# Layer 0's modulation products on VectorE among the convolution's passes, and a first norm whose shift is made by TensorE

## Chip, core and metric

One core of a Trainium2 chip runs the whole program. Its engines are TensorE (PE in the profile, its weight loads are PEld), VectorE (DVE), ScalarE (ACT), GpSimd (POOL) and SyncE (SP), which here issues almost all DMAs. The metric is the time of one execution on the device in microseconds. Lower is better.

## What is computed

An encoder block of two layers on one sequence of 1024 tokens with 1024 channels, all in float32. Layer 0 mixes tokens by a Conformer convolution, layer 1 by a gated linear recurrence in both directions; each mixer is followed by a squared-ReLU MLP. Every sub-layer is normalised first and then modulated: shift, scale and gate come from a conditioning vector `c`. Cut to what matters here:

```python
cond = silu(c)                                   # (1, 1024)
for i in range(2):
    mod = cond @ ada_w[i] + ada_b[i]             # 6 parts of 1024 numbers per layer
    sh1, sc1, g1, sh2, sc2, g2 = split(mod, 6)   # parts 0 to 5
    h = rms_norm(x, norm1_g[i]) * (1 + sc1) + sh1
    y = conformer_conv(h) if i == 0 else hgrn2_mixer(h)
    x = x + g1 * y
    h = rms_norm(x, norm2_g[i]) * (1 + sc2) + sh2
    x = x + g2 * sq_relu_mlp(h)
return rms_norm(x, final_g)

def conformer_conv(h):
    a, gate = split(h @ w_in, 2)                 # w_in (1024, 2048)
    y = depthwise_conv(a * sigmoid(gate), width=31) + dw_b
    return silu(layer_norm(y)) @ w_out
```

## The kernel before

`x` lies as 8 tiles of 128 channels by 1024 tokens; `s` counts the two halves of 512 tokens and `b` the 8 blocks of channels. Every large product is made of three TensorE products of operands split into a high and a low part (`hi` by ScalarE, `lo` = value minus `hi` by VectorE or GpSimd); the weights are split in the same way (`prep_std`, lines 206 and 208).

**Modulation.** `ada` makes one part: for each of 8 blocks it loads a tile of the transposed `ada_w` (128 outputs by 1024 inputs, 512 KB, line 409), multiplies it by `cond` spread over all partitions and sums along the row. With `eng="vector"` one VectorE instruction does both (line 412) and `ada_done` follows for that block: it adds the bias (line 436) and for the scales forms `AB` (line 441). With `eng="gpsimd"` GpSimd multiplies (line 415) and ScalarE sums (line 418).

**Start.** `start` makes `cond`, loads `x`, sums its squares (`stages`, lines 528 and 531, then token sums on TensorE, line 489), takes the inverse root by a few small VectorE instructions (`newton`, lines 460 to 471) and spreads it over the partitions (line 484). Scale (part 1) goes by VectorE, shift (part 0) by GpSimd and ScalarE but for its last block. Then for each `b` the first half of the tokens goes by lines 557, 565 and 566, the second by `mod_split_pool` (lines 574 to 578) with its low part on GpSimd. The first two weight splits of the convolution (`PW`) are on GpSimd too.

**Convolution.** `conv_layer` runs two passes over the tokens (`PASS`: five, then three token tiles of 128) with four groups of 256 channels each. In each (pass, group), `conv_in` has four steps, one for each quarter of the input channels; a step is 2 x 3 TensorE products of 512 columns for each token tile (lines 726 to 728, 0.23 us apart at full clock). Between the steps of one group stand `forward` (a DFT of the group before, lines 759 to 761, filter by VectorE in line 766, sums by GpSimd in line 768, splits in 288 and 289, result `Y`) and `backward` (line 784). `setup_late` loads and splits the DFT matrices into the space of `x` once `x` has been read. `conv_norm` is the layer norm and swish of one half (lines 801 to 837): it runs for the first half among the second pass, and for the second half among `out_proj`, which multiplies by `w_out` (lines 268 to 272) and adds to `x` (line 711). Parts 2, 4 and 3 of layer 0 are made by GpSimd and ScalarE, one block for each step from the second pass on and the rest in `out_proj`.

The order on each engine is worked out ahead by a scheduler that plays the program on a model of the engines and takes ready instructions by their place in the program; `keep_in_program_order` pins an instruction behind the one written before it on its engine. At run time each engine takes its list in order. The raw weight tiles, and the tiles of parts 2, 4 and 3, share four buffers (`raw`).

Of the kernel before, what the change touches and what calls it, by code (L numbers as in the profile page):

```python
# [6 lines left out]
F32 = mybir.dt.float32  # L7
# [6 lines left out]
P = 128  # L14
# [62 lines left out]
AW = 12  # L77

PW = [("ci", 0, 0, 0), ("ci", 0, 0, 1), ("co", 3), ("co", 4)]
# [12 lines left out]
class K:  # L92
# [226 lines left out]
    def setup_late(self):  # L319
# [7 lines left out]
        self.Gm = sp.tile([P, 2, 2, G], F32R, name="Gm")  # L327
        raw = None
        for i in range(n + 2):
            if i % 4 == 0:  # L330
                raw = self.raw()
                w = min(4, n + 2 - i) * G
                nc.sync.dma_start(out=raw[:, 0:w], in_=self.ins["dft"][:, i * G:i * G + w])
            src = raw[:, i % 4 * G:(i % 4 + 1) * G]
            hi, lo = (self.F[i][:, e].rearrange("p c f -> p (c f)") if i < n else self.Gm[:, e, i - n] for e in range(2))
            nc.scalar.copy(out=hi, in_=src)
            nc.vector.tensor_tensor(out=lo, in0=src, in1=hi.bitcast(F32), op=ALU.subtract)
# [10 lines left out]
    def load_masks(self):  # L348

        nc = self.nc  # L350
        self.masks = self.cp.tile([P, len(LEVELS), P], U8, name="masks")
# [30 lines left out]
    def cond_rows(self, bufs):  # L382
# [7 lines left out]
        for s in range(2):  # L390
# [4 lines left out]
            ps = self.aux()  # L395
# [5 lines left out]
    def ada(self, layer, part, cond, tile, eng="vector", late=False):  # L401

        nc = self.nc
        for b in range(NB):
            if layer == part == 0 and b == NB - 1:
                eng = "vector"
# [4 lines left out]
            if eng == "vector":  # L411
                nc.vector.scalar_tensor_tensor(out=raw, in0=raw, scalar=1.0, in1=cond, op0=ALU.mult, op1=ALU.mult,
                                               accum_out=m)
# [7 lines left out]
            if layer == part == 0:  # L421
                nc.scalar.activation(out=m, in_=m, func=AF.Identity, bias=self.adab[:, b:b + 1])
            elif eng == "vector" or layer == part // 2 == 0:
# [3 lines left out]
            if not late:  # L427
                yield

# [45 lines left out]
    def spread(self, r, bank=None):  # L475
# [5 lines left out]
        for j in range(n):  # L481
            c = slice(j * P, (j + 1) * P)
            nc.vector.tensor_scalar(out=d[:, c], in0=self.ident, scalar1=r[:, j:j + 1], scalar2=None, op0=ALU.mult)
            nc.tensor.matmul(out[:, c], self.ones_m, d[:, c], start=True, stop=True)
# [36 lines left out]
    def stages(self, srcs, npool=0, ps=None, bank=None):  # L521
# [4 lines left out]
        for i, x in enumerate(srcs):  # L526
            sq = self.qp.tile([P, H], F32, tag="sq", name=self.nm("sq"))[:, 0:n]
# [33 lines left out]
    def mod_split(self, layer, n, b, t, h=None):  # L561
        shift = self.gcol(layer, 3 * n, b)
        if h is None:
            h = self.hp.tile([P, 2, H], F32R, tag="h", name=self.nm("h"))
# [4 lines left out]

    def mod_split_pool(self, layer, n, s, b, r, h):  # L570

        nc = self.nc
        t = self.t512("h")
        nc.vector.scalar_tensor_tensor(out=t, in0=self.x[b][:, self.hs(s)], scalar=self.AB[:, layer, n, b:b + 1],
                                       in1=r, op0=ALU.mult, op1=ALU.mult)
        nc.scalar.activation(out=t, in_=t, func=AF.Identity, bias=self.gcol(layer, 3 * n, b))
        nc.scalar.copy(out=h[:, 0], in_=t)
        nc.gpsimd.tensor_tensor(out=h[:, 1], in0=t, in1=h[:, 0].bitcast(F32), op=ALU.subtract)
        return h
# [94 lines left out]
    def start(self):  # L674
# [3 lines left out]
        for s in range(2):  # L678
            self.load_x(s)
        ps = self.aux()  # L680
        for s in range(2):
            sums, _, _ = self.stages(self.xs(s), ps=ps[:, 4 * s:])
            sums()
        r = self.newton(ps, 8)
        rs = [self.spread(r[:, 4 * s:4 * s + 4]) for s in range(2)]
        tile = lambda: self.ada_tile(AW)
        g1, g0 = self.ada(0, 1, cond, tile, "vector"), self.ada(0, 0, cond, tile, "gpsimd")
        h = [[self.hp.tile([P, 2, H], F32R, tag="h", name=self.nm("h")) for _ in range(NB)] for _ in range(2)]

        def block(b):  # L690
            for s in range(2):
                if s:
                    self.mod_split_pool(0, 0, s, b, rs[s], h[s][b])
                else:
                    t, _ = self.mod_scale(0, 0, s, b, rs[s])
                    self.mod_split(0, 0, b, t, h[s][b])
        for b in range(NB):
            next(g1)
            next(g0)
            if b == 1:  # L700
                self.prep(1)
            if b >= 2:
                block(b - 2)
        for b in range(NB - 2, NB):
            block(b)
        self.fetch(3)
# [144 lines left out]
    def conv_layer(self, h):  # L851
        nc, tc = self.nc, self.tc
        z = [[], []]
        with tc.tile_pool(name="y", bufs=2 * NB) as self.yp:
            Y, S, U = [[], []], [[], []], {}
            norm = iter(())
            gen = None
            with tc.tile_pool(name="conv", bufs=1) as self.sp:
                self.setup_late()
                prev = None  # L860
                for ps in range(2):
                    for g in range(NG):
                        ci = self.conv_in(ps, g, h, U)

                        def go():
                            next(ci)
                            for _ in range(ps):
                                next(norm, None)
                            if ps and gen:
                                next(gen, None)  # L870
# [5 lines left out]
                        if prev:  # L876
                            self.backward(*prev, F, Y[prev[0]], S[prev[0]])
                            if prev == (0, NG - 1):
                                norm = self.conv_norm(Y[0], S[0], 0, z[0])
                                cond = self.cond_rows(0)  # L880
                                gen = itertools.chain(*(self.ada(0, part, cond, self.raw, "gpsimd") for part in (2, 4, 3)))
# [9 lines left out]
            with tc.tile_pool(name="convout", bufs=6) as self.sp:  # L891
# [6 lines left out]
                def step():  # L898
                    for _ in range(2):
                        with tc.high_priority():  # L900
                            next(norm, None)
                        next(gen, None)
# [3 lines left out]
                for _ in gen:  # L906
                    pass
# [598 lines left out]
    def rest(self, z):  # L1506
        tc, nc = self.tc, self.nc
        B = {}
        with tc.tile_pool(name="mlp0", bufs=1) as self.sp:
# [8 lines left out]
            def step(n):  # L1518
                if n >= 8 and n % 2 == 0:
                    next(gen, None)  # L1520
                if n == 7:
                    self.load_masks()
# [10 lines left out]
    def part2(self, h2):  # L1533
# [4 lines left out]
        with tc.tile_pool(name="hgrn", bufs=2) as self.sp:  # L1538
            z = self.hgrn_layer(h2)
# [16 lines left out]
def _arrays(inputs):  # L1556
# [7 lines left out]
    a["ada_t"] = np.ascontiguousarray(w.transpose(0, 2, 1)).reshape(2 * 6 * D, D)  # L1564
    a["dw"] = np.ascontiguousarray(inputs["conv_dw_w"][0])
# [37 lines left out]
```

## Time and profile before

| | |
|---|---|
| time, median of 3 runs | 2524.74 us (2520.14 to 2525.76) |
| time of the profiled execution | 2520.98 us |
| its span, first to last instruction | 2519.2 us |
| TensorE busy | 2405.6 us, 95% |
| VectorE busy | 1812.9 us, 72% |
| GpSimd busy | 1008.1 us, 40% |
| mean granted TensorE clock | 0.984 |

Busy time is a mean over stages with different limits. The change touches the first 430 us alone, in which TensorE is busy for 363.91 us; they are read in five stretches: up to the first product of the convolution (0 to 42 us), to the first `forward` (97), to the second pass (205), to the end of its last `conv_in` (332), and to where the MLP's first inputs are made (430).

### The profile page before, as it was taken

The page shows a single profiled execution, that of the slowest core. Times are in us where ns is not written, and L with a number is a line of the kernel's source. Part 1 is how long each engine was busy: PE and PEld are TensorE (multiplying, and loading weights), DVE is VectorE, ACT ScalarE, POOL GpSimd, SP SyncE. Part 2 cuts the span into 40 slices and gives each one's busy share as a digit, 9 for nine tenths or more (in the row PEclk, how much of TensorE's full clock was granted, in tenths as well). Part 3 has the DMA queues.
Part 4 walks back from the last instruction along what each step waited for, and adds up shares of the span by engine and source line. Part 5 has one row for each costly group of instructions (what it writes and reads, how often), then busy time and mean ns, then how long its engine had stood idle before and what let it go on. Part 6 is the DMA issues. An engine that isn't in the chain of part 4 may idle for free.

```text
span 2519.2 us, 32120 instructions
## 1 busy us (share of the span) xinstructions
PE 2405.6 (95%) x12024; PEld 2014.3 (80%) x12024; DVE 1812.9 (72%) x2440; ACT 1012.3 (40%) x1706; POOL 1008.1 (40%) x554
## 2 busy tenths in 40 slices
PE   4999998899999999999999999999989999999998
PEld 3788876677788778889898898988867888888887
DVE  8646778877676998756767867677579666695564
ACT  5424554433334344433434434343333333343443
POOL 4225673476664976012111111010036666474321
PEclk9999998999999999999999999999999999999999
DMA  6223473154547656541112211122523444664554
GB/s 253 91 67 104 131 267 134 35 189 161 167 147 278 246 200 235 175 155 59 59 51 76 67 43 59 59 68 84 205 71 138 142 155 160 218 249 175 184 185 150
DMA packets 217106, 358.62 MB, mean 142 GB/s; under 512 B 14005, under 2 KB 118612, under 8 KB 216950
## 3 DMA queue, kind: packets, MB, share of 16 engines
q1 hardware_dynamic: 215222, 354.48, 40.9%
q8 instruction: 94, 1.54, 0.2%
q10 hardware_dynamic: 1728, 2.10, 0.2%
q14 instruction: 62, 0.51, 0.1%
HBM read 278.92 MB, written 77.60 MB: 142 GB/s over the span
## 4 chain that ended last, share of the span: by engine, by line
PE 77%; DVE 9%; DMA 5%; POOL 4%; issue 4%; ACT 1%; SPq 0%; POOLq 0%; DVEq 0%; ACTq 0%
PE acc L281 17%; PE acc L964 5%; PE acc L965 5%; PE acc L960 5%; PE aux L1232 4%; PE acc L1061 4%; PE acc L1066 4%; PE acc L1065 4%; PE aux L1061 3%; PE aux L1066 3%; PE aux L1065 3%; PE aux L960 2%; PE aux L964 2%; PE aux L965 2%; POOL raw L415 2%
## 5 line engine op out<-in xcount | busy, mean ns | idle before, releaser
L415 POOL TENSOR_TENSOR raw<-raw,cond 128x1024 f32<-128x1024 f32 x56 | 157.1, 2807 | 548.6 <-DMA raw<-in_ada_t 343.7
L281 PE MATMUL acc<-h,wh 128*128 128x512 f32 x1024 | 328.6, 397 | 0.0
L236 DVE TENSOR_TENSOR wp<-raw,wp 128x512 fp32r<-128x512 f32 x192 | 204.3, 1071 | 104.5 <-ACT wp L235 103.6
L964 PE MATMUL acc<-h,wp 128*128 128x512 f32 x640 | 255.2, 399 | 10.0 <-DVE h L633 10.0
L960 PE MATMUL acc<-h,wp 128*128 128x512 f32 x640 | 252.5, 401 | 8.6 <-ACT wp L235 3.4
L235 ACT CAST wp<-raw 128x512 fp32r<-128x512 f32 x192 | 117.5, 621 | 347.3 <-PE acc L965 170.0
L965 PE MATMUL acc<-h,wp 128*128 128x512 f32 x640 | 251.7, 399 | 0.7 <-DVE wp L236 0.7
L281 PEld LDWEIGHTS acc<-h,wh 128*128 128x128 f32 x1024 | 189.7, 188 | 36.7
L1049 DVE TENSOR_TENSOR o<-hold,o 128x1024 fp32r<-128x1024 f32 x80 | 151.7, 1896 | 86.3 <-ACT o L1048 79.4
L281 PE MATMUL acc<-h,wl 128*128 128x512 f32 x512 | 202.5, 396 | 0.0
L1066 PE MATMUL acc<-o,o 128*128 128x512 f32 (+1 forms) x512 | 194.0, 380 | 2.9 <-DVE o L1049 2.9
L1061 PE MATMUL acc<-o,o 128*128 128x512 f32 (+1 forms) x512 | 195.2, 384 | 0.0
L1065 PE MATMUL acc<-o,o 128*128 128x512 f32 (+1 forms) x512 | 193.7, 379 | 0.0
L1049 DVE TENSOR_TENSOR o<-c,o 128x1024 fp32r<-128x1024 f32 x96 | 177.5, 1849 | 11.9 <-ACT o L1048 11.9
L208 DVE TENSOR_TENSOR wl<-raw,wh 128x1024 fp32r<-128x1024 f32 x84 | 114.2, 1360 | 90.8 <-ACT wh L206 87.5
L1061 PE MATMUL aux<-o,o 128*128 128x512 f32 (+1 forms) x448 | 171.6, 383 | 0.5 <-ACT o L1048 0.5
L1065 PE MATMUL aux<-o,o 128*128 128x512 f32 (+1 forms) x448 | 168.9, 377 | 0.0
L1066 PE MATMUL aux<-o,o 128*128 128x512 f32 (+1 forms) x448 | 166.2, 378 | 0.6 <-DVE o L1049 0.6
L206 ACT CAST wh<-raw 128x1024 fp32r<-128x1024 f32 x88 | 91.9, 1047 | 174.7 <-PE acc L281 116.5
L960 PEld LDWEIGHTS acc<-h,wp 128*128 128x128 f32 x640 | 122.1, 191 | 40.7 <-ACT wp L235 5.1
L964 PEld LDWEIGHTS acc<-h,wp 128*128 128x128 f32 x640 | 122.7, 192 | 38.9 <-DVE h L633 10.9
L1048 ACT CAST o<-hold 128x1024 fp32r<-128x1024 f32 x80 | 83.9, 1049 | 170.6 <-issue 86.4
(280 smaller groups left out, 6135.7 us busy)
## 6 DMA issues: line engine op xcount, KB each, us to landing
raw<-in_mlp_w SPq DMA_DIRECT2D x144, 512.0 KB, 4.6
c<-hid SPq DMA_DIRECT2D x112, 512.0 KB, 3.7
raw<-in_ada_t SPq DMA_DIRECT2D x80, 512.0 KB, 3.8
hid<-c SPq DMA_DIRECT2D x128, 256.0 KB, 3.1
hid<-t SPq DMA_DIRECT2D x96, 256.0 KB, 3.3
raw<-in_hgrn_w_in SPq DMA_DIRECT2D x40, 512.0 KB, 3.8
raw<-in_conv_w_in SPq DMA_DIRECT2D x64, 256.0 KB, 3.4
hold<-in_mlp_w SPq DMA_DIRECT2D x32, 512.0 KB, 7.8
```

The costliest lines, as they stand in the source:

```text
L208: eng.tensor_tensor(out=wl, in0=raw, in1=wh.bitcast(F32), op=ALU.subtract)
L235: nc.scalar.copy(out=hi, in_=a)
L236: nc.vector.tensor_tensor(out=lo, in0=a, in1=hi.bitcast(F32), op=ALU.subtract)
L281: m = self.nc.tensor.matmul(ps, a, b, start=(k == 0 and i == 0), stop=(k == n - 1 and i == 2))
L415: nc.gpsimd.tensor_tensor(out=raw, in0=raw, in1=cond, op=ALU.mult)
L960: m = nc.tensor.matmul(ps, wh, hi, start=(k == 0 and i not in (3, 6, 7)), stop=False, skip_group_check=True)
L964: nc.tensor.matmul(ps, wh, lo, start=False, stop=False, skip_group_check=True)
L965: nc.tensor.matmul(ps, wl, hi, start=False, stop=(k == KH - 1), skip_group_check=True)
L1049: nc.vector.tensor_tensor(out=lo, in0=src, in1=hi.bitcast(F32), op=ALU.subtract)
L1061: m = nc.tensor.matmul(ps[j], wh[:, c], hi, start=first, stop=False, skip_group_check=True)
L1065: nc.tensor.matmul(ps[j], wh[:, c], lo, start=False, stop=False, skip_group_check=True)
L1066: nc.tensor.matmul(ps[j], wl[:, c], hi, start=False, stop=stop, skip_group_check=True)
```

## The change

- Part 0 (shift) for the start is made by TensorE (`ada_pe`): `cond` as a column of one is the stationary operand, the untransposed `ada_w` streams past it in 16 products of 512 columns in float32; two rows come out, ScalarE copies them, eight small products turn them into columns, and one VectorE instruction adds the bias.
- Part 1 (scale) stays on VectorE, now pinned in program order, ahead of the shift.
- `mod_split_pool` goes; all low parts of the first norm are VectorE's. The tokens that the first pass doesn't need (384 of the second half) are done behind all that it needs.
- Parts 2, 4 and 3 go to VectorE: one block for each step from the second group of the first pass on (24 blocks, at an end in the third group of the second pass).
- The squares' scratch gets six buffers, the weight splits of the first two quarters go to VectorE, the inverse DFT matrix is kept at 172 columns, and the masks of layer 1 are loaded at its beginning.

```diff
-AW = 12
-PW = [("ci", 0, 0, 0), ("ci", 0, 0, 1), ("co", 3), ("co", 4)]
+AW = 8
+PW = [("co", 3), ("co", 4)]
...
+    def ada_pe(self, layer, part):
+        ps = [self.acc() for _ in range(2)]
+        for k in range(NB):
+            raw = self.ada_tile(0)
+            nc.sync.dma_start(out=raw, in_=self.ins["ada_w"][k * P:(k + 1) * P, :])
+            for j in range(2):
+                m = nc.tensor.matmul(ps[j][0:1], self.cond[:, k:k + 1], raw[:, self.hs(j)],
+                                     start=(k == 0), stop=(k == NB - 1))
+                self.tc.keep_in_program_order(m)
+        rows = []
+        for j in range(2):
+            row = self.t512("row")[0:1]
+            nc.scalar.copy(out=row, in_=ps[j][0:1])
+            rows += [row[:, i * P:(i + 1) * P] for i in range(4)]
+        cols = self.aux()
+        for b in range(NB):
+            nc.tensor.matmul(cols[:, b:b + 1], rows[b], self.ones_c[0:1], start=True, stop=True)
+        self.ada_done(layer, part, cols[:, 0:NB], 0, NB)
...
     def start(self):
+        scale = self.ada(0, 1, cond, lambda: self.ada_tile(AW), "vector")
...
-        rs = [self.spread(r[:, 4 * s:4 * s + 4]) for s in range(2)]
-        tile = lambda: self.ada_tile(AW)
-        g1, g0 = self.ada(0, 1, cond, tile, "vector"), self.ada(0, 0, cond, tile, "gpsimd")
+        rs = [self.spread(r[:, 4 * s:4 * s + 4], pin=True) for s in range(2)]
+        for _ in scale:
+            pass
+        self.ada_pe(0, 0)
...
+        first = (PASS[0].stop - 4) * P
+        self.prep(0)
+        parts = [(b, s, c) for b in range(NB) for s, c in ((0, slice(0, H)), (1, slice(0, first)))]
+        parts += [(b, 1, slice(first, H)) for b in range(NB)]
+        for n in range(len(parts) + 3):
+            if n < len(parts):
+                ts.append(scale(*parts[n]))
+            if n >= 3:
+                split(*ts[n - 3])
+            if n % 4 == 3 and n < 2 * NB:
+                self.prep(n // 4 + 1)
...
     def conv_layer(self, h):
+                cond = self.sp.tile([P, D], F32, name="condc")
+                nc.sync.dma_start(out=cond, in_=self.kept.broadcast_to([P, D]))
+                gen = itertools.chain(*(self.ada(0, part, cond, self.raw, "vector") for part in (2, 4, 3)))
...
                             next(ci)
+                            for _ in range(1 if ps or g else 0):
+                                next(gen, None)
                             for _ in range(ps):
                                 next(norm, None)
-                            if ps and gen:
-                                next(gen, None)
...
-                                cond = self.cond_rows(0)
-                                gen = itertools.chain(*(self.ada(0, part, cond, self.raw, "gpsimd") for part in (2, 4, 3)))
...
     def part2(self, h2):
         with tc.tile_pool(name="hgrn", bufs=2) as self.sp:
+            self.load_masks()
             z = self.hgrn_layer(h2)
```

## Rows read from the trace of the kernel before

**Rows 1.** Windows: time; PE, PEld, DVE, ACT, POOL busy (instructions); clock, DMA share, GB/s.
```profile
0.00:42.00 42.00, 10.77 (x35) 7.91 (x36) 33.43 (x63) 20.68 (x34) 16.05 (x10) 1.00 0.95 347
42.00:97.00 55.00, 45.90 (x166) 33.40 (x165) 47.66 (x71) 34.26 (x69) 19.79 (x11) 0.91 0.29 99
97.00:205.00 108.00, 108.00 (x594) 93.91 (x593) 44.40 (x69) 33.17 (x58) 22.77 (x24) 1.00 0.20 64
205.00:332.00 127.00, 114.49 (x637) 98.45 (x635) 96.41 (x121) 63.50 (x112) 79.96 (x53) 0.96 0.43 142
332.00:430.00 98.00, 84.75 (x369) 67.73 (x370) 82.24 (x114) 46.58 (x76) 57.41 (x35) 0.91 0.57 198
```
**Rows 2.** Whom TensorE waited for, 0 to 130: us, times, longest.
```profile
PE acc L728 <- DVE h L566: 8.4, 4, 3.9
```
**Rows 3.** The same, 205 to 332 (first row) and 332 to 430 us.
```profile
PE aux L784 <- DVE Y L289: 7.3, 4, 4.2
...
PE mu L489 <- DVE sq L818: 4.8, 1, 4.8
PE acc L268 <- ACT z L288: 3.4, 1, 3.4
```
**Rows 4.** GpSimd by line and form, 200 to 420: busy, mean ns; idle, releaser.
```profile
L415 POOL TENSOR_TENSOR raw<-raw,aw 128x1024 f32<-128x1024 f32 x24 | 66.7, 2785 | 48.1 <-DMA raw<-in_ada_t 38.1 <-DVE sg L837 5.3 <-DVE u L734 4.6
L768 POOL TENSOR_TENSOR p<-p,q 128x256 f32<-128x256 f32 x30 | 24.8, 859 | 2.4 <-DVE q L766 2.4
```
**Rows 5.** VectorE by line, 97 to 205 (two rows), 205 to 332 (two), 332 to 430.
```profile
L208 DVE TENSOR_TENSOR wl<-raw,wh 128x1024 fp32r<-128x1024 f32 x12 | 14.7, 1224 | 32.6 <-ACT wh L206 32.6
L766 DVE TENSOR_TENSOR q<-aux,W 128x512 f32<-128x512 f32 x9 | 6.1, 681 | 0.0
...
L208 DVE TENSOR_TENSOR wl<-raw,wh 128x1024 fp32r<-128x1024 f32 x16 | 28.7, 1795 | 7.1 <-ACT wh L206 7.1
L766 DVE TENSOR_TENSOR q<-aux,W 128x512 f32<-128x512 f32 x12 | 8.2, 680 | 1.4 <-POOL p L768 1.4
...
L815 DVE TENSOR_TENSOR sq<-sq,sq 128x512 f32<-128x512 f32 x4 | 9.1, 2285 | 0.1
```
**Rows 6.** Timeline of VectorE and GpSimd: start us, us, what.
```profile
20.29 5.17 POOL L415 TENSOR_TENSOR aw<-aw,cond 128x1024 f32<-128x1024 f32 x2 [19.84 <-DMA aw<-in_ada_t]
...
23.17 2.30 DVE L436 TENSOR_TENSOR mod<-mod,adab 128x1 f32<-128x1 f32 x1
...
51.52 3.39 DVE L412 SCALAR_TENSOR_TENSOR aw<-aw,cond 128x1024 f32<-128x1024 f32 x1
54.84 0.15 DVE L436 TENSOR_TENSOR mod<-mod,adab 128x1 f32<-128x1 f32 x1
...
55.57 1.22 DVE L412 SCALAR_TENSOR_TENSOR aw<-aw,cond 128x1024 f32<-128x1024 f32 x1
...
58.75 0.73 DVE L557 SCALAR_TENSOR_TENSOR h<-x,AB,aux 128x512 f32<-128x512 f32 x1
```
**Rows 7.** Timeline of TensorE and ScalarE, 0 to 90 us.
```profile
6.96 3.78 PE L396 MATMUL aux<-silu,ones_m 1*128 1x512 f32 x4 [6.96 <-DVE silu L394]
...
11.51 0.57 ACT L397 COPY cond<-aux 128x512 f32<-128x512 f32 x1
...
26.13 1.86 PE L489 MATMUL aux<-ones_d,sq 128*128 128x1 f32 x8 [10.00 <-DVE sq L531]
...
38.74 3.75 PE L484 MATMUL aux<-d,ones_m 128*128 128x128 f32 x16 [10.75 <-DVE d L483]
...
41.80 0.72 ACT L565 ACTIVATE h<-h,mod 128x512 fp32r<-128x512 f32 x1 [14.04 <-DVE h L557]
...
42.58 0.79 PE L726 MATMUL acc<-wh,h 128*128 128x512 f32 x1
...
44.76 0.39 PE L727 MATMUL acc<-wl,h 128*128 128x512 f32 x1
...
81.84 2.81 PE L345 MATMUL aux<-raw,fw 31*128 31x512 f32 x6 [0.55 <-DMA fw<-in_fw]
```

## What the trace of before says the change will do

> **What bounds the kernel.** I read the windows first. The reader is to see that TensorE sets the pace, and where it falls short of its own pace. The loss of a stretch is its length less TensorE's busy time, plus (1 - granted clock) times its length, since work at half clock takes double. From [rows 1]: 42 to 97 us loses 9.1 + 0.09 x 55 = 14 us; 97 to 205 nothing; 205 to 332 loses 12.5 + 0.04 x 127 = 18; 332 to 430 loses 13.3 + 0.09 x 98 = 22. With the 42 us of the start, in which TensorE works for 10.8, that is all that this change can give back or spoil. Second, the waits: in the first norm TensorE waits for VectorE's low parts [rows 2], in the second pass for `Y`, in the second layer norm for the sum of squares and `z` [rows 3]. VectorE is late, so third, what makes it late: GpSimd by line [rows 4], where the modulation (L415) is 66.7 us in 24 instructions. In [rows 5] the reader compares one instruction in two stretches: L208 takes 1.22 us where GpSimd works 21% of the time and 1.80 where it works 63%; the squares (L815) take 2.29 in the last stretch, for as many elements as L766, which takes 0.68. Fourth, the timeline [rows 6] shows it one by one: a VectorE instruction on a single column takes 2.30 us behind a GpSimd product and 0.15 without one; the modulation product takes 3.39 or 1.22.
>
> The Trainium skill, SBUF — State Buffer, section "Who interferes with whom", has the rule: VectorE and GpSimd share a pair of ports that one instruction holds to its end, if VectorE's reads two operands from SBUF. The trace agrees: L766, with one operand in PSUM, takes 0.68 us in both stretches [rows 5].
>
> **The change, part by part.**
>
> *The start.* Removed: seven products and eight low parts on GpSimd, and on ScalarE the sums and second passes. ScalarE is busy for half of those 42 us [rows 1] and sets nothing there; I credit it with nothing.
>
> When can TensorE begin? DMA first: `x`, eight tiles of scale and eight of shift are 12.6 MB as before, at 347 GB/s with engines 95% busy [rows 1] 36 us. The bytes are the same, so no gain; the last shift tile lands at about 37, the first at about 28. SP's queue has the convolution's weights behind them, where before four of these stood among them; their splits (1.22 each on VectorE [rows 5]) fit in before the shift is ready, and cost nothing; if the first doesn't, about 2 us. The eight tiles of the scale (buffers 12 to 8) are just those in flight. The token sums, the root and the spread come earlier, since VectorE loses its stalls: I put the end of the spread at 26 instead of 42.5 (`x` is 4.2 MB, landed at about 15, and the last adds end at 19; then 1.9 for token sums, some 1.5 for a dozen small instructions of the root, and 3.75 for the spread [rows 6, 7]).
>
> Then the new work. A float32 product of 512 columns is two records: L345, with as many columns and 31 rows, takes 2.81 us for three products, 0.94 each; L396, with one row, 3.78 us for two, 1.9 each, at the low clock [rows 7]. So 16 products are 15 us at the high clock and 30 at the low one. With tiles 1.5 us apart they are held by TensorE, not by DMA. Which end? Before the convolution TensorE ran L484 and its first products from 38.74 at a low clock and was at full pace at 44.76 [rows 7], about 6 us later. I take 5 us at the low clock and the rest at the high one: 2.6 products, then 13.4 x 0.94 = 12.6, so 17.6 us; from 28 to 45.6. Behind it, in series: two copies of 0.57, eight small products (L489: four for 1.86 us at the low clock [rows 7], so 1.9 to 3.7; I take 2.5), the bias (0.15), the shifted high part (0.72), and about 1 us of handovers: 5.5 us. The first product of the convolution comes at 51 instead of 42.58.
>
> That is later, but it then runs on. Before, the work of 42 to 97 takes 55 - 14 = 41 us, so it ends as if it had begun at 56 and never waited. After, VectorE has 12 us of scale products (eight of 1.22 with their small ones) done before 51, and lies ahead with scaled tiles and weights. From then until `forward` it has eight times four instructions of the part that the first pass needs, the rest of the second half behind them, the weights, the DFT matrices and `u`: some 35 us against 38 of TensorE, after what it did in advance. The eight low parts that come to it are 8 x 0.73 = 6 us [rows 6], and cutting the second half in two adds 16 instructions at 0.15 (the fixed part, as L436) or more, 2.4 us; both are in that 35, hidden by TensorE's 41 us, and cost up to 8 us if that cover goes. With 2 us of first waits the work ends as if begun at 53: **3 us gained**. Bounds: all at the high clock begins at 48 and gains 7; all at the low clock begins at 64 and loses 10.
>
> *The 24 products in the passes.* Each is 1.22 us of VectorE and its small adds 0.15 [rows 6], 1.37 in all, 33 us. Twelve fall in the first pass, where VectorE is busy for 44.4 of 108 us [rows 1] and waits 32.6 us for weights alone [rows 5]: cost nothing. Twelve fall in 205 to 332, 16.5 us. There VectorE's 96.4 us hold some 19 us of stalls (16 times 0.57 for L208 alone [rows 5]); without them 77, and GpSimd's share of modulation was nearly half of its 80 us, so about 10 of the 19 stay: 77 + 16.5 + 10 = 104 us, against TensorE's 109 of work. VectorE is no longer slack there. What is gained: `Y` isn't behind a modulation product on GpSimd any more (7.3 us of waits [rows 3]). What is lost: it may be behind one of 1.22 on VectorE. I take **2 us gained**, between 8 gained and 8 lost. Queues: SP issues these 24 loads earlier, among the weights; each keeps one of four `raw` buffers for its landing and 1.2 us instead of its landing, GpSimd's 2.8 [rows 4] and ScalarE's sum, and DMA is 20% busy in the first pass [rows 1]; nothing. The scheduler's other choices are in the range.
>
> *The second layer norm.* In 332 to 430 GpSimd loses ten products, 28 of its 57 us [rows 1, 4]. VectorE, 82 us busy, has about 20 us of stalls there (four L815 alone 6.4 [rows 5]); half go. This chain is what TensorE waits for (4.8 and 3.4 us [rows 3], and the clock of 0.91 behind them), so I give **10 us**, between 4 and 18 (nearer the middle, since GpSimd keeps its own squares and two weight splits).
>
> *The rest.* The narrower inverse matrix saves 0.1 us twice. The masks, one DMA and one cast, go to a place where TensorE is 100% busy: nothing, 4 us if the scan waited for them.
>
> Sum: 3 + 2 + 10 = 15 us off the profiled execution's 2521 us: **2506 us**. That execution is 3.8 us below the median of the runs, so this is 0.7% below the median; 0.2%, 5 us, is about what a measurement of this kernel can tell from no change.
>
> **Rivals.**
>
> *The shift stays at the low clock.* All 16 products at 1.9 us [rows 7]: the start loses 10, the rest gives 12, **2519 us**. For it: L396, L489 and L484, all before 42 us, ran low. Against: dense products then did reach the high one. Chance 0.20. The Trainium skill, TensorE: Matmul & The Clock Gate, section "What's actually happening", has the throttled clock as the default which activity releases; no row shows whether products with one stationary column do so.
>
> *VectorE bounds the second pass.* Its 104 us come in lumps, and TensorE's losses there grow by 8 instead of falling: 2521 - 3 + 8 - 10 = **2516 us**. For it: 104 of 109; against: 7.1 us of that stretch VectorE waits on ScalarE anyway [rows 5]. Chance 0.15.
>
> *Slower: each product holds TensorE.* The 24 products stand ahead of work that is due just then (`Y`, weights) and each delays TensorE by its 1.37 us: 33 us against the 3 + 2 + 10 and the 5 more of the `Y` waits: 2521 - 20 + 33 = **2534 us**. From 15 of the 24 on it decides against the change. Against: VectorE's idle time in the first pass. Chance 0.14. By the rule on the shared ports each of them also locks out GpSimd's L768, which feeds `Y`; for that the trace has no row with a product on VectorE, only the reverse.
>
> **Numbers.** My sum has 0.51; its own range is 2496 to 2514. Faster by over 0.2% (below 2520): the sum, most of the second rival and half of the first, 0.70. Same: the rest of these, 0.15. Slower: 0.15. Range 2490 to 2527: it takes in the first two rivals and nearly all bounds of the terms at once on the fast side (7 + 8 + 18 is 2488), and leaves the slow one out.
>
> **What would show it.** The profile after should show: L415 gone before 430 us; the shift's products from 28 to 46, at 0.94 after the first few (1.9 throughout is the first rival); the first convolution product near 51 and no wait on low parts after it; VectorE's small instructions back at 0.15 in the start; L815 in the second norm below 1.5 us; `Y` waits in the second pass under 5 us (above 12: the second or third rival). I am wrong if `forward` of the first group comes later than 97, or if the second norm's chain isn't shorter.

## The result, and the profile after

The changed kernel takes 2493.76 us in the median of 4 runs (2492.47 to 2495.68), the kernel before on the same chip 2525.25 us (2520.14 to 2526.18). The ratio is 0.988, with a 95% interval of 0.9863 to 0.9897: 31 us, 1.2% faster. The forecast was 2506 us (2490 to 2527). Direction and range hold; the gain is about twice the 15 us that the sum gave. The profiled execution after took 2495.68 us with a span of 2493.9 us, so from profile to profile the gain is 25.3 us; the profiled execution of before was one of its quicker ones.

The windows of the kernel after, cut at its own landmarks (time; PE, PEld, DVE, ACT and POOL busy; clock, DMA share, GB/s):

```profile
0.00:48.00 48.00, 28.56 (x84) 12.70 (x84) 34.33 (x91) 20.98 (x32) 0.20 (x4) 1.00 0.95 345
48.00:95.00 47.00, 45.34 (x168) 33.00 (x169) 35.93 (x76) 24.47 (x53) 0.00 (x0) 0.89 0.33 109
95.00:200.00 105.00, 105.00 (x579) 91.39 (x578) 62.54 (x112) 31.36 (x57) 25.20 (x23) 1.00 0.38 125
200.00:315.00 115.00, 107.08 (x615) 92.99 (x614) 91.40 (x147) 50.52 (x83) 41.09 (x37) 0.97 0.41 130
315.00:425.00 110.00, 105.21 (x504) 86.20 (x504) 81.51 (x131) 42.49 (x68) 32.67 (x24) 1.00 0.42 148
```

The reader sees three things against [rows 1]. From the first product of the convolution on TensorE idles little: by the prediction's own measure (idle time plus what the clock takes) the stretches lose 7, 0, 11 and 5 us, where they lost 14, 0, 18 and 22. The last stretch has a clock of 1.00 instead of 0.91. For the third, the stretches have to hold the same work: from the last `conv_in` to the first product of the MLP, first before and then after:

```profile
321.00:449.40 128.40, 113.67 (x506) 91.56 (x505) 97.75 (x131) 55.52 (x94) 68.10 (x41) 0.93 0.52 185
...
312.00:421.60 109.60, 104.81 (x505) 85.97 (x504) 81.39 (x130) 43.52 (x70) 34.00 (x26) 1.00 0.45 155
```

TensorE and VectorE each have the same number of instructions in both, but for one. GpSimd's busy time halves, VectorE's falls by 16 us with all of its work but one small instruction left, and TensorE's loss falls from 24 us to 5.

The table gives the starts of some instructions in both traces; the last column is what the changed kernel has gained by then.

| | before, us | after, us | gained |
|---|---|---|---|
| first product of the convolution | 42.6 | 48.1 | -5.5 |
| first `forward` | 96.6 | 94.6 | 2.0 |
| last product of `conv_in` | 321.2 | 312.0 | 9.2 |
| last `backward` | 348.4 | 331.7 | 16.7 |
| first product of the MLP | 449.4 | 421.6 | 27.8 |
| end of the span | 2519.2 | 2493.9 | 25.3 |

Of the gain 2 us are there at the first `forward`, 7.2 come up to the last `conv_in`, 18.6 up to the MLP, and 2.5 are lost behind it, where no run looks for the reason.

The timeline of TensorE in the start (start us, us, what, idle time before), whole instructions of the shift and the first of the convolution:

```profile
24.29 3.78 PE L503 MATMUL aux<-d,ones_m 128*128 128x128 f32 x16 [2.80 <-DVE d L502]
29.59 15.40 PE L436 MATMUL acc<-aw,cond 128*1 128x512 f32 x32 [1.52 <-DMA aw<-in_ada_w]
44.92 1.94 PE L446 MATMUL aux<-ones_c,row 1*128 1x1 f32 x16
48.15 0.50 PE L746 MATMUL acc<-wh,h 128*128 128x512 f32 x1 [1.29 <-ACT h L712]
```

Its 32 records in two windows, cut where their pace changes:

```profile
29.59:32.80 3.21, 3.21 (x4) 0.47 (x5) 3.07 (x10) 0.00 (x0) 0.00 (x0) 1.00 1.03 410
32.80:44.99 12.19, 12.19 (x30) 2.34 (x28) 8.03 (x19) 3.71 (x4) 0.00 (x0) 1.00 1.04 368
```

Four records take 3.21 us, 0.80 each; the other 28 (two records of the small products are counted too) take 12.2, 0.43 each. So two products of 512 columns ran at half pace and fourteen at 0.87 us. The clock column is 1.00 in both windows and doesn't show this change of pace; the lengths of the records do.

Whom TensorE waited for, in the second pass (200 to 315) and behind it (315 to 425), us in all, times, longest:

```profile
PE acc L746 <- DVE u L754: 3.9, 2, 3.6
PE aux L804 <- DVE Y L289: 1.7, 2, 1.4
PE aux L804 <- ACT Y L288: 1.5, 1, 1.5
PE mu L510 <- DVE sq L838: 0.8, 1, 0.8
...
PE aux L503 <- DVE d L502: 3.1, 1, 3.1
PE acc L271 <- POOL z L289: 1.0, 2, 0.8
PE acc L271 <- DVE z L289: 0.7, 1, 0.7
```

Of the long waits of [rows 3] `Y` fell from 7.3 us to 1.7 and `z` from 3.4 to under 2. The wait for the sum of squares, 4.8 us in the norm of the second half, is gone; the 0.8 listed stands in the norm of the first half. The longest single wait is now one for `u` (3.6 us), which in the second pass before took 1.6 us in one wait. Of the waits for the first norm's low parts [rows 2] none is left.

VectorE by line, 95 to 200 (first row), 200 to 315 (two), 330 to 430 (one): busy, mean ns; idle, releaser.

```profile
L410 DVE SCALAR_TENSOR_TENSOR raw<-raw,condc 128x1024 f32<-128x1024 f32 x12 | 14.8, 1236 | 30.1 <-DMA raw<-in_ada_t 30.0
...
L208 DVE TENSOR_TENSOR wl<-raw,wh 128x1024 fp32r<-128x1024 f32 x16 | 22.2, 1388 | 4.3 <-ACT wh L206 4.3
L410 DVE SCALAR_TENSOR_TENSOR raw<-raw,condc 128x1024 f32<-128x1024 f32 x9 | 13.1, 1452 | 15.8 <-DMA raw<-in_ada_t 15.8
...
L835 DVE TENSOR_TENSOR sq<-sq,sq 128x512 f32<-128x512 f32 x4 | 4.4, 1107 | 0.2
```

Three more products stand before 95 us, so 15 of the 24 are done ahead of the second pass. The same 16 weight splits take 1.39 us on average, where they took 1.80, and the four squares 1.11 instead of 2.29 [rows 5].

### The profile page after: what moved, and what is told of

Same layout as the page of the kernel before. It is cut to its first block, busy times and chain, and to the rows that moved or that the text cites. A ratio compares the mean times of both kernels' runs of the same rounds, so it can differ in the third digit from the quotient of the medians.

```text
span 2493.9 us, 32162 instructions
## 1 busy us (share of the span) xinstructions
PE 2408.6 (97%) x12072; PEld 2009.6 (81%) x12072; DVE 1801.6 (72%) x2545; ACT 978.6 (39%) x1638; POOL 904.5 (36%) x508
## 4 chain that ended last, share of the span: by engine, by line
PE 81%; DVE 8%; DMA 4%; POOL 3%; issue 3%; ACT 1%; SPq 0%; POOLq 0%; DVEq 0%; ACTq 0%
PE acc L281 17%; PE acc L982 5%; PE acc L983 5%; PE acc L978 5%; PE aux L1250 4%; PE acc L1079 4%; PE acc L1084 4%; PE acc L1083 4%; PE aux L1079 3%; PE aux L1084 3%; PE aux L1083 3%; PE acc L268 2%; PE acc L271 2%; PE acc L272 2%; PE aux L978 2%
```

## The experiments

All are edits of the changed kernel, e2 alone of the one before; each time is the median of 4 or 5 runs, and each ratio is to the kernel before on the same chip (2525.0 to 2525.8 us).

**The two halves of the change.** e1 keeps the new start and puts the 24 products back where they were, on GpSimd and ScalarE; e2 keeps the old start and takes the new passes.

```diff
-                gen = itertools.chain(*(self.ada(0, part, cond, self.raw, "vector") for part in (2, 4, 3)))
...
+                                cond = self.cond_rows(0)
+                                gen = itertools.chain(*(self.ada(0, part, cond, self.raw, "gpsimd") for part in (2, 4, 3)))
...
-                            for _ in range(1 if ps or g else 0):
-                                next(gen, None)
...
+                            if ps and gen:
+                                next(gen, None)
...
```

Both keep the narrower inverse matrix and the moved masks.

> The changed kernel's start alone: parts 2, 4 and 3 go back to GpSimd and ScalarE, from the second pass on and in the output projection, as before. Mine (most of the gain comes from GpSimd's modulation leaving the second pass and the second layer norm): the first forward stands near 95 us instead of 97, the rest as before, so 2521 to 2524 us. Rival (the start carries the change, since TensorE then runs without gaps): 2500 to 2508.

> The start of before, with GpSimd and ScalarE in it, and parts 2, 4 and 3 on VectorE among the passes as in the changed kernel. Mine: nearly all of the 31 us, 2495 to 2502. Rival (the start carries it): 2515 to 2522. If the parts add up, this one's gain and that of the start alone together give 31 us.

e1: 2517.27 us, 0.9965 [0.9952, 0.9978]. e2: 2504.5 us, 0.9913 [0.9895, 0.9931]. Both lie outside the range that was expected, e1 by 4 us on the fast side and e2 by 2.5 on the slow one. The start alone is worth 8 us, the passes alone 21; together 29 of the 31 us, so within the intervals the halves add up. Most of the gain is the products'.

**Engine and place of the products.** In e3 they stand at the new places, but on GpSimd with ScalarE (`"vector"` becomes `"gpsimd"` in the line that makes `gen`); in e4 on VectorE, at the old places (e1's edit with `"vector"`).

> The changed kernel with the 24 products of parts 2, 4 and 3 at the same early places, but made by GpSimd with ScalarE's sums instead of VectorE. If the place is what counts (the products are gone from the second layer norm): 2494 to 2500. If the engine counts (GpSimd's product locks VectorE out and stands ahead of GpSimd's sums for Y): back to 2510 to 2520. Mine is between: the second layer norm's share of the gain, some 17 us, stays, the second pass's 6 us goes, the first pass has slack: 2498 to 2506.

> The changed kernel with the 24 products on VectorE, but at the places of before: one for each step of the second pass, eight more in the output projection beside the second layer norm. If the engine alone counts: 2494 to 2500. Mine: VectorE is full there, eight times 1.37 us and their waits for the tiles come back into the chain of the second layer norm, 2503 to 2512. If the place alone counts: 2515 or more.

e3: 2500.43 us, 0.9901 [0.9887, 0.9916]. e4: 2509.19 us, 0.9936 [0.9921, 0.9951]. With e1 and the changed kernel that is a square, all with the new start:

| | old places | new places |
|---|---|---|
| GpSimd and ScalarE | 2517.3 (e1) | 2500.4 (e3) |
| VectorE | 2509.2 (e4) | 2493.8 (changed kernel) |

The place is worth 17 us on GpSimd and 15 on VectorE, the engine 8 and 7. So a story by the engine alone falls: GpSimd at the new places has all of the gain but 7 us. What the new places have is seen in [rows 1]: in the first pass VectorE is busy for 44.4 of 108 us. At the old ones its time is short, and both ways of doing a product there take time from it, its own work in e4 (33.4 us for 23 products from 200 to 430 us), GpSimd's in e1. The windows from 315 to 425 us (columns as above) show it, first of e1:

```profile
315.00:425.00 110.00, 95.31 (x437) 76.91 (x436) 88.80 (x118) 52.80 (x88) 65.62 (x40) 0.92 0.59 205
```

of e4, with TensorE's longest wait in them:

```profile
315.00:425.00 110.00, 99.66 (x463) 81.12 (x464) 93.49 (x161) 41.50 (x66) 36.32 (x25) 0.94 0.59 201
...
PE acc L268 <- DVE sg L857: 7.4, 1, 7.4
```

and of e3:

```profile
315.00:425.00 110.00, 105.21 (x506) 86.34 (x505) 81.44 (x130) 44.22 (x72) 35.10 (x26) 1.00 0.47 160
```

In e1 GpSimd is at its busiest (65.6 us), in e4 VectorE (93.5); TensorE idles 15 and 10 us and its granted clock is 0.92 and 0.94. In e3 neither is, and TensorE has the 105.21 us at 1.00 of the changed kernel.

**How GpSimd takes time from VectorE.** e13 is e1 with each of the 24 products replaced by two fills of the same tile, which read nothing; e14 has three fills each. (The rest of the edit is e1's.)

```diff
-                nc.gpsimd.tensor_tensor(out=raw, in0=raw, in1=cond, op=ALU.mult)
+                if layer == 0 and part in (2, 4, 3):
+                    for _ in range(2):
+                        nc.gpsimd.memset(raw, 0.0)
+                else:
+                    nc.gpsimd.tensor_tensor(out=raw, in0=raw, in1=cond, op=ALU.mult)
```

> The run with the changed start alone, with each of the 24 products on GpSimd replaced by two fills of the same tile, which keep GpSimd about as busy at the same places but read nothing; ScalarE's sums stay, so parts 2, 4 and 3 are left out of the result. If VectorE loses its time to the ports that GpSimd holds while it reads: the squares of the second layer norm fall from 2 us to below 1.2 and 2503 to 2510. If it is GpSimd's own queue that is late for its sums and squares: 2514 to 2519.

> The kernel of e13_late_memsets with three fills in place of each of the 24 late products on GpSimd instead of two (parts 2, 4 and 3 of layer 0 are left out, as there). In e1 the 24 products kept GpSimd busy for 63.5 us, in e13 48 fills kept it busy for 45.5; 72 fills of 0.95 us are 68 us, a little more than the products. So GpSimd's own list is as full as in e1, and only what the instructions read differs. Theory that GpSimd's reading holds VectorE (ports): 2496 to 2503 us, the squares of the second norm near 1.1 us and the weight splits of the second pass near 1.3 us, as in e13. Theory that GpSimd's list is the matter (its sums for the filter and its low parts come late): 2510 to 2518 us, as e1, with more waits for the filter's sums than in e13. In between: each has its share, and the difference to e13's 2495.9 is that of the list.

e13: 2495.87 us, 0.9877 [0.9848, 0.9906]. e14: 2494.64 us, 0.9879 [0.9862, 0.9895]. The rows that decide are GpSimd's line from 200 to 420 us, VectorE's weight splits from 200 to 330 and its squares from 330 to 430, first in e1:

```profile
L415 POOL TENSOR_TENSOR raw<-raw,aw 128x1024 f32<-128x1024 f32 x24 | 63.5, 2651 | 43.0 <-DMA raw<-in_ada_t 39.9 <-DVE z L289 3.0
...
L208 DVE TENSOR_TENSOR wl<-raw,wh 128x1024 fp32r<-128x1024 f32 x16 | 31.5, 1970 | 8.9 <-ACT wh L206 8.8
...
L835 DVE TENSOR_TENSOR sq<-sq,sq 128x512 f32<-128x512 f32 x4 | 9.2, 2288 | 0.1
```

and then in e14:

```profile
L417 POOL MEMSET raw<- 128x1024 f32 x70 | 66.0, 958 | 25.6 <-DMA raw<-in_ada_t 18.7 <-DVE d L506 4.7 <-DVE rw L487 0.7
...
L208 DVE TENSOR_TENSOR wl<-raw,wh 128x1024 fp32r<-128x1024 f32 x15 | 19.9, 1326 | 13.8 <-ACT wh L206 13.7
...
L839 DVE TENSOR_TENSOR sq<-sq,sq 128x512 f32<-128x512 f32 x4 | 4.7, 1187 | 0.1
```

GpSimd is as busy in this line, 66.0 us against 63.5, and VectorE's splits and squares fall to 1.33 and 1.19 us from 1.97 and 2.29. The time falls by 22.6 us, to the level of the changed kernel. e13 is below both of its expected ranges, e14 just below the range of the first theory. So it isn't GpSimd's full list that costs the time, but what its instructions do to VectorE's. One thing more differs: a fill is shorter than a product, 0.96 us against 2.65, so it could hold VectorE in the same way and only let it go sooner. The timeline of e14 speaks against that. First VectorE, then GpSimd for the same microseconds:

```profile
342.64 0.68 DVE L839 TENSOR_TENSOR sq<-sq,sq 128x512 f32<-128x512 f32 x1
343.25 1.21 DVE L208 TENSOR_TENSOR wl<-raw,wh 128x1024 fp32r<-128x1024 f32 x1
...
344.98 1.77 DVE L557 TENSOR_TENSOR sq<-sq,sq 128x512 f32<-128x512 f32 x1
...
340.85 3.65 POOL L417 MEMSET raw<- 128x1024 f32 x4
344.46 1.75 POOL L839 TENSOR_TENSOR sq<-sq,sq 128x512 f32<-128x512 f32 x1
```

In the midst of four fills a square takes 0.68 us and a weight split 1.21, as in a quiet stretch [rows 5]. Beside the next GpSimd instruction, which reads, an add of squares of the same size takes 1.77. So of VectorE's instructions with two operands only GpSimd's readers hold up any. The rule of the Trainium skill, SBUF — State Buffer, section "Who interferes with whom", says just this: a VectorE instruction with two SBUF inputs contends with a GpSimd instruction that reads SBUF, and not with one that only writes it. e1 and e14 agree with it, in the rows above. What isn't held fixed is the order of the instructions: it is worked out anew for each kernel, so it differs too, and its share of the 22.6 us is not shown.

**What the 24 products cost on VectorE.** In e8 they go over 2 of the 1024 columns; loads and buffers stay.

```diff
-                i = nc.vector.scalar_tensor_tensor(out=raw, in0=raw, scalar=1.0, in1=cond, op0=ALU.mult, op1=ALU.mult,
+                c = slice(0, D if part == 1 else 2)
+                i = nc.vector.scalar_tensor_tensor(out=raw[:, c], in0=raw[:, c], scalar=1.0, in1=cond[:, c], op0=ALU.mult, op1=ALU.mult,
```

> The changed kernel with the 24 products of parts 2, 4 and 3 over 2 of 1024 columns: some 25 us of VectorE less, their DMAs and waits kept. If VectorE's work hides in its idle time, as the first rival-free sum had it: 2489 to 2494. If every product holds TensorE (the slower rival of the prediction): 2468 to 2475.

2490.45 us, 0.9865 [0.985, 0.9879]: 3 us below the changed kernel, with intervals that overlap, for 24 us of VectorE's busy time less (24 products in 7.5 us instead of 31.6). The products are hidden nearly to the last, and TensorE isn't held by them.

**The price of the shift.** In e6 it has one tile and two products instead of eight and sixteen.

```diff
-        for k in range(NB):
+        for k in range(1):
             raw = self.ada_tile(0)
...
-                                     start=(k == 0), stop=(k == NB - 1))
+                                     start=(k == 0), stop=(k == 0))
```

> The changed kernel with the shift made from the first 128 of the 1024 inputs only (one tile and two products instead of eight and 16), which prices the shift on TensorE with its DMAs. Theory: the first product comes at about 40, when the last scale is there, and up to 8 us are gained: 2486 to 2490. Rival (VectorE sets the first group): 2491 to 2495.

2485.29 us, 0.9843 [0.9828, 0.9858]. The first product of the convolution comes at 40.8 instead of 48.1 and the end 8.5 us earlier. That is the most that a better place for the shift could still give, since e6 also saves seven of its eight loads and most of its time on TensorE.

**Earlier shift, two attempts.** e5 and e10 load the shift's tiles ahead of the scale's and put its products ahead of the root and the spread. In e5 VectorE's bias add for the shift is also ahead of the scale's products in its order; in e10 it is behind them. The edit shown is e10's; in `ada_pe` the loads, the products and the bias become three parts, run by `next`.

```diff
+        shift = self.ada_pe(0, 0)
+        next(shift)
         scale = self.ada(0, 1, cond, lambda: self.ada_tile(AW), "vector")
...
+        next(shift)
         r = self.newton(ps, 8)
...
         for _ in scale:
             pass
-        self.ada_pe(0, 0)
+        next(shift)
```

> The changed kernel with the shift's tiles loaded ahead of the scale's and its 16 products ahead of the spread, so that they run while the scale's tiles still land. Theory (the serial shift behind the scale's DMAs sets the first product of the convolution at 48 us): first product at 42 to 44 us and 3 to 5 us off the changed kernel's 2494, so 2489 to 2491. Rival (VectorE, busy all of 50 to 70 us, sets the first group): the first product is earlier and the first forward is not, 2493 to 2496.

> The run with the shift first, with one order mended: there the shift's bias stood on VectorE ahead of the scale's products and held them from 26 to 41 us; here it stands behind them. Theory (TensorE's serial shift behind the scale's DMAs sets the first product, and VectorE must have the scale done by then): first product at 43 to 45 us, first forward near 91, 2489 to 2492. Rival (the first group is VectorE's anyway): forward at 94 or later, 2493 to 2497.

e5: 2502.77 us, 0.9907 [0.9891, 0.9924], 9 us worse than the changed kernel. VectorE's timeline in e5 shows why:

```profile
24.89 0.87 DVE L508 TENSOR_SCALAR d<-ident,rw 128x128 f32<-128x128 f32 x4
41.30 0.17 DVE L461 TENSOR_TENSOR mod<-aux,adab 128x8 f32<-128x8 f32 x1 [15.54 <-PE aux L451]
41.38 1.22 DVE L410 SCALAR_TENSOR_TENSOR aw<-aw,cond 128x1024 f32<-128x1024 f32 x1
```

For 15.5 us VectorE stands before an add of 0.17 us, with the scale's products queued behind it; the first `forward` comes at 103.4, 9 us late. e10: 2495.48 us, 0.9882 [0.9867, 0.9897]. There the first product comes at 43.9 and the first `forward` at 85.3, 9 us earlier than in the changed kernel, and yet it isn't faster; neither of its forecasts has an early `forward` without a gain. Part of the 9 us is order and no lead: ahead of that `forward` TensorE has done 139 products of `conv_in` in e10 and 156 in the changed kernel, and 17 products at 0.23 us are 4 us. The windows of e10 show where the rest goes:

```profile
95.00:200.00 105.00, 102.97 (x545) 88.48 (x545) 60.77 (x109) 31.51 (x57) 23.76 (x23) 0.98 0.36 120
200.00:315.00 115.00, 107.99 (x613) 93.51 (x613) 92.34 (x151) 50.99 (x85) 41.74 (x37) 0.97 0.42 135
```

TensorE, without idle time from 95 to 200 us in the changed kernel, waits 2.0 us there in e10, and the clock of 0.98 takes some 2 more. With the 4 us of order that is 8 of the 9, and the norm's first token sums stand at 219.9 us, 1.5 ahead of the changed kernel. Behind 315 us the granted clock is 0.97 in e10 and 1.00 in the changed kernel, 3 us over those 110, so the last of the lead is gone too. Why the clock is lower there stays open.

**The loads of the products.** In the changed kernel VectorE stands 47.2 us in 19 waits before products whose tile hasn't landed, and one of these holds `u`, and with it TensorE, for 3.65 us up to 256.56. e7 loads each tile one step ahead; e11, whose edit is shown, also pins the product in its place.

```diff
+        load(0)
+        yield
+        for n, (part, b) in enumerate(items):
+            load(n + 1)
...
+            i = nc.vector.scalar_tensor_tensor(out=raw, in0=raw, scalar=1.0, in1=cond, op0=ALU.mult, op1=ALU.mult,
+                                               accum_out=m)
+            self.tc.keep_in_program_order(i)
```

> The changed kernel with each tile of parts 2, 4 and 3 loaded one step before the step of its product. In the changed kernel VectorE stands 47 us in 19 waits with such a product at the head of its queue, its tile not landed. Theory (these waits hold up what is queued behind, as the 3.7 us wait for u at 253 us): 3 to 8 us gained, 2486 to 2491. Rival (TensorE is covered but for that once, and a buffer held longer delays the weights): 2493 to 2500.

> The run with loads a step ahead left VectorE's waits for the tiles at 48 us, as the scheduler moved each product up with its load. Here each product is pinned behind what stands before it on VectorE, a step after its load. If the waits at the head of VectorE's queue cost time: waits for the tiles under 15 us and 2488 to 2491. Rival (they are idle time of VectorE that TensorE covers): waits under 15 us and 2492 to 2497.

e7: 2493.03 us, 0.9873 [0.9858, 0.9887], with the waits as before (48.4 us, 20 times): the scheduler moves the product up along with its load. e11: 2493.89 us, 0.9875 [0.986, 0.989]. VectorE's longest waits from 48 to 345 us in e11:

```profile
DVE wl L208 <- ACT wh L206: 32.6, 18, 10.8
DVE u L778 <- ACT u L777: 27.0, 11, 6.5
DVE p L810 <- PE aux L805: 10.5, 4, 3.6
```

The waits for tiles are gone, others have taken their place, and the time is the same. TensorE's wait for `u` falls from 3.9 us to 2.0, but its waits for `Y` rise from 3.2 to 4.6. So nearly all of VectorE's idle time there was slack.

## Why the prediction was right, and where its sizes were off

The time lies in the stated range, but the sum does not carry it there. The sum was 15 us; measured are 25 from profile to profile and 31 in the median, and its own range of 2496 to 2514 us is missed by 2 us. What held was the direction, the mechanism and the wide range.

**The start** was forecast at 3 us. The products of the shift ran from 29.6 to 45 (forecast 28 to 45.6), at 0.87 us but for the first two (0.94 after 2.6), and the first product of the convolution came at 48.1 (forecast 51), since the chain behind the shift took 3.2 us and not 5.5. At the first `forward` 2.0 us were gained, or 2.9 by the work done, as four more products of `conv_in` (0.9 us) are behind TensorE by then. That it would begin later and then wait little was right; that the 3 us came out is in part luck. TensorE began 3 us sooner than forecast, and then lost 7 us, where the prediction had 2: 1.7 of idle time and 5 of clock. The granted clock falls behind TensorE's wait for the DMA of `fw` (1.5 us, up to 76.25; windows as above):

```profile
75.00:80.00 5.00, 3.75 (x6) 1.54 (x7) 3.95 (x8) 4.56 (x12) 0.00 (x0) 0.70 0.34 113
80.00:85.00 5.00, 5.00 (x9) 2.42 (x9) 4.42 (x10) 3.58 (x8) 0.00 (x0) 0.50 0.62 215
```

The prediction had no term for the clock there. (Its fast bound of 7 us is 6 by its own sum, as the 2 us of first waits stay.) By medians e1 gives 8 us for the start (5.5 to 12 by its interval), by the two spans 3.0 (2519.2 to 2516.2); the difference is the quick execution of before that was profiled, and a slower one of e1.

**The second pass** was forecast at 2 us, and 7.2 were gained from the first `forward` to the last `conv_in`. Two numbers in that term were wrong. Twelve products were put into the pass, but 9 ran there. And "about 10 of the 19 us of stalls stay" with VectorE at 104 of 109 us: it was busy for 91.4 of 115, and the splits' share fell from 0.57 to 0.17 us each. The `Y` waits shrank, as said. The wait that a product puts ahead of `u` (3.6 us) comes from a tile that hadn't landed, and the loads were put at nothing; e11 takes that wait away and gains nothing, so the size is right, but not because no product stands waiting.

**The second layer norm** was forecast at 10 us, between 4 and 18. From the last `conv_in` to the MLP 18.6 us were gained, just above the upper bound. This is the term that was most undersized, and the step that was mis-sized is "half go", with a value "nearer the middle" because GpSimd keeps other work. The mechanism was right: the squares came under 1.5 us, the waits for them and for `z` went, and the clock of 0.91 became 1.00. But VectorE's busy time fell by 16 us for the same work, where 10 of about 20 us of stalls were to go, with GpSimd still busy for 34 us, and TensorE's loss went from 24 us to 5. (It was nine products that GpSimd lost behind 332 us, 25.3 us, and not ten with 28; the term doesn't hang on that.) One us of stalls was taken for one us of time, and that about came out (16 and 18.6). e1 against e14 shows 22.6 us, from the second pass on, that go with GpSimd's reads.

**Put at nothing**: the products' own time in the first pass. By e8 all 24 products together cost about 3 us, within both intervals; the loads, by e11, nothing.

**The rivals.** The shift at the low clock: refuted by the records from 32.8 us on. VectorE as the bound of the second pass: 91.4 of 115 us, and `Y` waits of 3.2 us with ScalarE's. Each product holding TensorE for 1.37 us: e8 takes 24 us from VectorE, and TensorE gets 3 back. It would have been nearer the truth at the old places: e4 is 15 us slower than the changed kernel.

What was not seen ahead is that the place does twice as much as the engine. The prediction told the change as one of engines, and costed the move into the first pass only as "nothing"; that it frees the second layer norm wholly, on either engine, is what e3 showed.

## What to carry to other kernels

A side job goes where the engine it disturbs has slack, and that includes an engine that it only locks out: first the place, then the engine. Where two engines share a way into memory, look at one instruction's mean time in a busy and in a quiet stretch; the excess in a serial chain, here a layer norm, was given back nearly whole, and the clock behind it too. An earlier start or shorter waits on an engine with slack gave nothing that these runs can tell (e10, e7, e11), and one small instruction put too early in an engine's order cost 9 us (e5).

## What the hardware showed that was not expected

The products with a stationary operand of one column ran at 0.80 us a record for 3.2 us and then at 0.43: TensorE's clock rose while nothing but such products ran. The Trainium skill, TensorE: Matmul & The Clock Gate, section "What's actually happening", has activity release a throttled default; the trace agrees, by these two lengths. In three runs the clock that the convolution finds goes with the idle time before it, and not with the run of shift products alone:

```profile
40.79 0.79 PE L746 MATMUL acc<-wh,h 128*128 128x512 f32 x1 [5.41 <-ACT h L712]
...
43.90 1.65 PE L755 MATMUL acc<-wh,h 128*128 128x512 f32 x3 [3.14 <-ACT wh L206]
```

The first row is from e6, with two of these products and 5.41 us of idle time, the second from e10, with all sixteen and 3.14 us. In both the products behind the first came 0.43 us apart; in the changed kernel, with all sixteen and 1.29 us, 0.23 apart: 1.2 and 2.4 GHz.

VectorE's waits on GpSimd aren't quite gone in the changed kernel. These are rows of VectorE's timeline in the root of the norm ahead of the MLP, and below them GpSimd's for the same microseconds, which splits a block of `z` and combines blocks of the MLP's weights (L240):

```profile
381.46 1.23 DVE L479 TENSOR_SCALAR rw<-rw 128x4 int32<-128x4 int32 x1
382.73 1.22 DVE L480 TENSOR_SCALAR rw<-rw 128x4 int32<-128x4 int32 x1
...
387.67 0.16 DVE L482 TENSOR_TENSOR rw<-rw 128x4 f32<-128x4 f32 x1
```

```profile
381.37 1.29 POOL L289 TENSOR_TENSOR z<-sg,z 128x512 fp32r<-128x512 f32 x1 [1.94 <-ACT z L288]
382.62 2.54 POOL L240 TENSOR_TENSOR s<-raw,raw 128x512 f32<-128x512 f32 x2
385.12 2.50 POOL L240 TENSOR_TENSOR raw<-raw 128x512 f32<-128x512 f32 x2
```

Five instructions on four columns, of which two have a single operand (L479, L480), take 1.2 us each as long as GpSimd works, 0.16 behind it: some 5 us on the way to the MLP's first product, and TensorE idles for 3.1 us before the spread that follows. Five such instructions stand in the kernel before as well (407.8 to 414.0 us), so the change neither made nor mended this.

Instructions on a single tile wait where those on two don't. Beside e14's fills, which read nothing, a bit shift on four columns and the four instructions that prepare the spread (a tile times one scalar for each partition) take:

```profile
354.51 1.05 DVE L483 TENSOR_SCALAR rw<-rw 128x4 int32<-128x4 int32 x1
...
357.57 1.73 DVE L506 TENSOR_SCALAR d<-ident,rw 128x128 f32<-128x128 f32 x4
```

Without GpSimd they take 0.17 and 0.88 us in the changed kernel (356.27 and 388.93 us). The same section of the Trainium skill, SBUF — State Buffer, "Who interferes with whom", names one-operand forms too, if they run in a mode of two ports. These rows fit that; in which mode these instructions run, no run shows. What moving the GpSimd instructions would give was not tried.
